# Weight-sum transfers of the seven-product groups, placed at written-out chunks of the load stream

## The chip, the cores and the metric

The kernel runs on one NeuronCore of a Trainium2 chip. The metric is the device time of one execution in microseconds (us). The engines that matter are TensorE (PE in the profile: matrix products and transposes), VectorE (DVE), ScalarE (ACT), GpSimd (POOL) and SyncE (SP). SP issues nearly all loads, POOL issues a few DMAs and computes the small powers of the norms. Each engine executes its own instructions in the order in which they were written, and waits for others by semaphores.

## The reference

Two decoder layers on 256 tokens of width 1024, all in float32. Layer 0 has a short gated convolution, attention over a memory of 256 rows, and a SwiGLU block; then one shared key and value projection. Layer 1 has block-sparse attention with these keys and values (with 256 tokens there is one block, so it is causal attention), memory attention, and SwiGLU.

```python
def mem_cross_attention(h, mem_n, w_q, w_kv, w_o):
    q = (h @ w_q).reshape(bsz, seq, MEM_HEADS, MEM_HEAD_DIM)
    k, v = jnp.split(mem_n @ w_kv, 2, axis=-1)
    ...
    return o @ w_o

def swiglu(h, w_gu, w_down):
    g, u = jnp.split(h @ w_gu, 2, axis=-1)
    return (jax.nn.silu(g) * u) @ w_down

def reference(...):
    for l in range(DEPTH):
        h = rms_norm(x, norm_mix[l])
        ...                      # short_conv_mixer or moba_attention, added to x
        x = x + mem_cross_attention(rms_norm(x, norm_mem[l]), rms_norm(mem, norm_memkv[l]), ...)
        x = x + swiglu(rms_norm(x, norm_ffn[l]), ffn_w_gu[l], ffn_w_down[l])
    return rms_norm(x, norm_final)
```

## The kernel before

**Products.** Every float32 product is made of three matmuls in a reduced format: each operand is split into a rounded part (hi) and the rest (lo), and lo x hi, hi x lo and hi x hi are added up in PSUM. Weights arrive as chunks of 128 x 1024 (512 KB). For each chunk SP loads raw_NAME, ACT casts it to hi_NAME, DVE subtracts to lo_NAME, and TensorE uses both. Names give the stage: memk, memv, mq and mo are the memory attention's key, value, query and output weights, k1, q1, v1 and o1 those of layer 1's attention, wr the row-wise pairs of the gate and up projection, wg, wu and wd its other pieces. There are five raw buffers (RAWS) and ten pairs of hi and lo (WBUFS), so the load of chunk n waits until lo of chunk n-5 is done.

**The load stream.** All chunks stand in one list, numbered from 0. Around the change: mo0 56 to 63, wr0 64 to 71, wg0 from 72; k1 136 to 143, q1 144 to 151, v1 152 to 159, memk1 160 to 167, o1 168 to 175, memv1 176 to 183, mq1 184 to 191, mo1 192 to 199, wr1 200 to 207, wg1 from 208. `Feed.load_to` issues the loads in this order, and just before chunk n it runs the functions that stand in `feed.hooks[n]`.

**What sets the order of the casts.** The kernel is written out by a planner, the class `Clock`. It holds one time for each engine and one for the DMA engines, and estimates when every tile is ready. `Feed.pump` is called between matmuls; it emits the hi cast of the next chunk on ACT (`split_high`) when the planner's time says that the raw chunk has landed and ACT is free, and then the lo subtraction on DVE (`split_low`). If `take` needs a chunk whose casts are not yet written, they are written there. So the planner's times decide nothing on the chip but the order of instructions on each engine.

**The sums.** Three of the eleven 256-wide pieces of the feed-forward layers (piece 8 of layer 0, pieces 4 and 8 of layer 1) are computed with seven products of quarter blocks in place of eight. For each, four sums of quarter blocks of the weight (T1 to T4, each in two parts i) are formed in DRAM by DMAs, in 16 steps: T1 <- B11, T3 <- B12 (plain copies), T1 += B12, T3 += B22 (accumulating DMAs), T2 <- T1 (copy), T2 += B22, T4 <- T2 (copy), T4 += B21. The plain copies are issued by SP (line 553), the accumulating ones by POOL (line 551). They are used much later, as chunks raw_wT. Each step also moves the planner's DMA time on, by 1460 ns for a copy and 3300 ns for an accumulate:

```python
            def run():
                clock.free["dma"] = max(clock.free["dma"], clock.now)
                if add:
                    nc.gpsimd.dma_start(dst, src, accum_op=OP.add, max_dma_last_dim=8192)
                else:
                    nc.sync.dma_start(dst, src)
                clock.note("dma", 3300 if add else 1460, [], [])
```

The steps are spread by `SUMS_AT` (loop at line 1041): the 16 of layer 0 evenly over chunks 44 to 104, the 32 of layer 1 evenly from chunk 128 on, the last ones drawn in to chunk 210.

Lines that the trace names: 242 is the helper that records every ACT, DVE and POOL operation, 464 the matmul, 468 the transpose, 481 the load of a chunk, 551 and 553 the accumulate and the copy of a sum, 1641 the load of the memory's transposed rows (mT, kept aside in DRAM, issued by POOL), 763 the first tile used to warm TensorE up.

Of the kernel before, what the change touches and what calls it, by code (L numbers as in the profile page):

```python
# [43 lines left out]
LATER = 2000  # L44
BANKWISE = 5
GROUPS = ((8,), (4, 8))
SUMS_AT = ((44, 104, 104), (128, 220, 210))


class Rows:  # L50
# [348 lines left out]
def yoco_kernel(  # L399
# [135 lines left out]
    def sum_steps(l, jp):  # L535
        for name in ("T1", "T2", "T3", "T4"):
            for i in range(2):
                weight_sums[l, jp, name, i] = aside.tile([P, 2, 2 * T], F32, name=f"{name}_{l}_{jp}_{i}")

        def step(name, source, i, add):  # L540
            dst = weight_sums[l, jp, name, i]
            if source[0] == "T":
                src = weight_sums[l, jp, source, i]
            else:
                n = quarters[l, jp, source, i]
                src = chunks[n * P:(n + 1) * P].rearrange("p (a n) -> p a n", a=2)
# [9 lines that stand above are left out]
            return run  # L556

        order = (("T1", "B11", False), ("T3", "B12", False), ("T1", "B12", True), ("T3", "B22", True),
                 ("T2", "T1", False), ("T2", "B22", True), ("T4", "T2", False), ("T4", "B21", True))
        return [step(name, source, i, add) for name, source, add in order for i in range(2)]  # L560

    plan, _, quarters, ffn_steps = weight_plan()
    feed = side.feed = Feed(clock, plan, load_chunk, split_high, split_low)
# [475 lines left out]
        feed.hooks[36 + k] = [put_aside(k)]  # L1039

    for l in range(2):
        steps = [step for jp in GROUPS[l] for step in sum_steps(l, jp)]
        first, end, last = SUMS_AT[l]
        for n, step in enumerate(steps):
            at = min(first + (end - first) * n // len(steps), last + n - len(steps))
            feed.hooks.setdefault(at, []).append(step)


    def short_conv(act, into):
# [711 lines left out]
```

## Time and profile before

| what | value |
|---|---|
| three runs | 783.0, 783.08, 783.8 us (median 783.08) |
| profiled execution | 783.51 us |
| its span, first to last instruction | 781.7 us |
| mean granted TensorE clock | 0.998 |
| DMA, mean over the span | 234 GB/s, 182.71 MB |
| accumulates of sums (POOL), each | 512 KB, 7.6 us from issue to landing, 24 of them |
| copies of sums (SP), each | 512 KB, 7.1 us (from the weights) and 5.4 us (T from T), 12 of each |

The page is read from the busy times down: which engine is nearly always busy, what it waited for, and then the stretches (windows of 10 us) in which the moved work lies. A row of the timeline gives start, duration, engine, line, operation, output and inputs, the count of instructions drawn together (the duration is then that of all), and in brackets the idle time before it with what ended it. Rows overlap slightly, since an instruction may start before the one ahead has written everything back.

### The profile page before, as it was taken

How to read it: one execution, taken by the hardware profiler on the slowest of the kernel's cores; microseconds unless marked ns; L12 is line 12 of the kernel's file. 1: busy time of each engine (PE TensorE's matmuls, PEld its weight loads, DVE VectorE, ACT ScalarE, POOL GpSimd, SP SyncE). 2: the span in 40 equal slices, each digit the busy share in tenths (PEclk: the TensorE clock that was granted, in tenths of full speed). 3: DMA queues.
4: the chain of work that ended last, by engine and by line, in shares of the span. 5: the costliest groups of instructions: out<-in, count | busy, mean ns of one | idle time of the engine just before them, and what ended most of it. 6: DMA issues, size and time to landing. Idle time of an engine off the chain costs nothing.

```text
span 781.7 us, 11230 instructions
## 1 busy us (share of the span) xinstructions
PE 773.4 (99%) x4147; PEld 665.0 (85%) x4147; DVE 573.6 (73%) x872; ACT 458.8 (59%) x728; POOL 36.8 (5%) x68
## 2 busy tenths in 40 slices
PE   9999999999999999999999999999999999999996
PEld 8988888898888888888888889888988888888885
DVE  6988888768786566687766566876867876966964
ACT  6875665665654555566564563655756556655741
POOL 1000011000100000000110010030000000000000
PEclk9999999999999999999999999999999999999999
DMA  9776888916676755699787556899674646946931
GB/s 345 277 275 214 275 287 230 372 67 212 193 245 232 226 174 205 207 366 330 217 306 243 188 161 218 294 266 310 208 224 151 241 158 226 321 164 211 345 111 54
DMA packets 48807, 182.71 MB, mean 234 GB/s; under 512 B 6256, under 2 KB 7280, under 8 KB 46576
## 3 DMA queue, kind: packets, MB, share of 16 engines
q1 hardware_dynamic: 45968, 166.79, 59.7%
q0 software_dynamic: 2208, 14.68, 9.2%
q8 instruction: 32, 0.52, 0.3%
q10 hardware_dynamic: 576, 0.52, 0.2%
q14 instruction: 23, 0.19, 0.1%
HBM read 178.82 MB, written 28.31 MB: 265 GB/s over the span
## 4 chain that ended last, share of the span: by engine, by line
PE 95%; DVE 1%; issue 0%; ACT 0%; POOLq 0%; DVEq 0%; ACTq 0%
PE gu L464 17%; PE ff L464 15%; PE seven L464 7%; PE q_acc L464 6%; PE cu L464 6%; PE rows L464 6%; PE acc_mo L464 6%; PE acc_memv L464 6%; PE acc_memk L464 4%; PE pb L464 3%; PE acc_v L464 3%; PE acc_q L464 3%; PE acc_o L464 3%; PE acc_cout L464 3%; PE acc_k L464 3%; PE po L464 2%
## 5 line engine op out<-in xcount | busy, mean ns | idle before, releaser
L464 PE MATMUL ff<-hi_wd,guT 128*128 128x512 f32 (+1 forms) x352 | 108.2, 388 | 0.0
L464 PEld LDWEIGHTS ff<-hi_wd,guT 128*128 128x128 f32 x352 | 65.8, 188 | 12.8
L464 PE MATMUL ff<-lo_wd,guT 128*128 128x512 f32 (+1 forms) x176 | 68.3, 388 | 0.0
L242 DVE TENSOR_TENSOR gu_sb<-gu_sb,gu 128x256 f32<-128x256 f32 x48 | 19.9, 421 | 58.7 <-ACT gu_sb L242 58.0
L242 DVE TENSOR_TENSOR lo_wd<-raw_wd,hi_wd 128x1024 fp32r<-128x1024 f32 x44 | 53.5, 1221 | 2.9 <-ACT hi_wd L242 2.7
L242 ACT COPY gu_sb<-gu 128x256 f32<-128x256 f32 x48 | 17.8, 372 | 61.4 <-PE gu L464 61.3
L242 ACT CAST hi_wd<-raw_wd 128x1024 fp32r<-128x1024 f32 x44 | 46.1, 1050 | 11.3 <-DMA raw_wd<-in_chunks_dram 9.4
L464 PE MATMUL gu<-ffn,hi_wg 128*128 128x512 f32 x192 | 48.0, 390 | 0.0
L464 PE MATMUL gu<-ffn,hi_wu 128*128 128x512 f32 x192 | 47.6, 390 | 0.0
L464 PE MATMUL acc_memk<-mT,hi_memk 128*128 128x256 f32 x256 | 44.3, 291 | 0.0
L242 ACT CAST hi_wu<-raw_wu 128x1024 fp32r<-128x1024 f32 x32 | 33.5, 1051 | 15.2 <-DMA raw_wu<-in_chunks_dram 10.9
L464 PEld LDWEIGHTS gu<-ffn,hi_wg 128*128 128x128 f32 x192 | 35.9, 188 | 7.3
L464 PEld LDWEIGHTS gu<-ffn,hi_wu 128*128 128x128 f32 x192 | 35.8, 188 | 7.3
L464 PE MATMUL rows<-hi_wr,ffn 128*128 128x512 f32 x128 | 40.7, 395 | 0.0
L464 PE MATMUL acc_mo<-hi_mo,oT_mem 128*128 128x512 f32 x128 | 40.6, 393 | 0.0
L464 PE MATMUL acc_memv<-hi_memv,mT 128*128 128x512 f32 x128 | 39.6, 390 | 0.0
L242 DVE TENSOR_TENSOR lo_wu<-raw_wu,hi_wu 128x1024 fp32r<-128x1024 f32 x32 | 38.9, 1221 | 0.6 <-ACT hi_wu L242 0.5
L464 PEld LDWEIGHTS acc_memk<-mT,hi_memk 128*128 128x128 f32 x256 | 38.8, 199 | 0.4 <-ACT hi_memk L242 0.3
L464 PEld LDWEIGHTS ff<-lo_wd,guT 128*128 128x128 f32 x176 | 33.2, 188 | 6.2
L242 POOL TENSOR_TENSOR rs<-ms,neg_half 128x1 f32<-128x1 f32 x14 | 13.5, 964 | 436.6 <-DVE ms L242 420.2
L464 PE MATMUL q_acc<-mem,hi_mq 128*128 128x512 f32 x128 | 32.4, 394 | 0.0
L242 DVE TENSOR_TENSOR lo_wg<-raw_wg,hi_wg 128x1024 fp32r<-128x1024 f32 x24 | 28.7, 1221 | 4.0 <-ACT hi_wg L242 3.9
(277 smaller groups left out, 1954.6 us busy)
## 6 DMA issues: line engine op xcount, KB each, us to landing
raw_wd<-in_chunks_dram SPq DMA_DIRECT2D x44, 512.0 KB, 4.9
raw_wu<-in_chunks_dram SPq DMA_DIRECT2D x32, 512.0 KB, 5.0
T<-in_chunks_dram POOLq DMA_DIRECT2D x24, 512.0 KB, 7.6
raw_wg<-in_chunks_dram SPq DMA_DIRECT2D x24, 512.0 KB, 5.0
raw_wT<-T SPq DMA_DIRECT2D x24, 512.0 KB, 4.7
raw_wB<-in_chunks_dram SPq DMA_DIRECT2D x18, 512.0 KB, 5.0
raw_memv<-in_chunks_dram SPq DMA_DIRECT2D x16, 512.0 KB, 4.7
raw_mq<-in_chunks_dram SPq DMA_DIRECT2D x16, 512.0 KB, 6.0
```

The lines of the kernel that those rows point to most:

```text
L242: return call(out, *args, **kw)
L464: nc.tensor.matmul(o, l, r, start=start, stop=stop)
```

## The change

`SUMS_AT` becomes a table of chunk numbers, one for each of the 16 steps of a group, and the loop reads it.

```diff
-SUMS_AT = ((44, 104, 104), (128, 220, 210))
+SUMS_AT = {
+    (0, 8): (65,) * 8 + (74, 77, 81, 85, 89, 92, 96, 100),
+    (1, 4): (128, 131, 134, 137, 140, 143, 146, 148) + (159,) * 4 + (166,) * 4,
+    (1, 8): (168,) * 8 + (201, 201, 202, 202, 206, 207, 208, 209),
+}
...
     for l in range(2):
-        steps = [step for jp in GROUPS[l] for step in sum_steps(l, jp)]
-        first, end, last = SUMS_AT[l]
-        for n, step in enumerate(steps):
-            at = min(first + (end - first) * n // len(steps), last + n - len(steps))
-            feed.hooks.setdefault(at, []).append(step)
+        for jp in GROUPS[l]:
+            for at, step in zip(SUMS_AT[l, jp], sum_steps(l, jp)):
+                feed.hooks.setdefault(at, []).append(step)
```

In layer 0 the first eight steps of piece 8 (four copies, four accumulates) now stand together before chunk 65. In layer 1 the second half of piece 4 stands before chunks 159 and 166, and the first eight steps of piece 8 before chunk 168. Lines shift by four in the changed kernel (242 becomes 246, 464 becomes 468, 481 becomes 485, 551 and 553 become 555 and 557).

On SP, around the first chunks of wr0, the order was this (the last two loads of mo0, then wr0; a number behind a name counts tiles):

```order
L481 DMA raw_mo0_6_1747<-in_chunks_dram 128x1024 [waits DMAHW1_49,DVE_49]
L481 DMA raw_mo0_7_1806<-in_chunks_dram 128x1024 [waits DMAHW2_49,DVE_49]
L481 DMA raw_wr0_0_0_1851<-in_chunks_dram 128x1024 [waits DMAHW3_49,DVE_49,Activation_49]
L481 DMA raw_wr0_0_1_2045<-in_chunks_dram 128x1024 [waits DMAHW5_49,DVE_49,Activation_49]
L481 DMA raw_wr0_0_2_2099<-in_chunks_dram 128x1024 [waits DMAHW6_49,DVE_49,Activation_49]
```

and is now this:

```order
L485 DMA raw_mo0_7_1800<-in_chunks_dram 128x1024 [waits DMAHW6_49,DVE_49]
L485 DMA raw_wr0_0_0_1845<-in_chunks_dram 128x1024 [waits DMAHW7_49,DVE_49,Activation_49]
L557 DMA T1_0_8_0_495<-in_chunks_dram 16x8192
L557 DMA T1_0_8_1_496<-in_chunks_dram 16x8192
L557 DMA T3_0_8_0_499<-in_chunks_dram 16x8192 [waits DMAHW0_49]
L557 DMA T3_0_8_1_500<-in_chunks_dram 16x8192 [waits DMAHW1_49]
L485 DMA raw_wr0_0_1_2047<-in_chunks_dram 128x1024 [waits DMAHW2_49,DVE_49,Activation_49]
L485 DMA raw_wr0_0_2_2100<-in_chunks_dram 128x1024 [waits DMAHW3_49,DVE_49,Activation_49]
```

The four copies, which stood between earlier loads, now stand behind the first load of wr0.

On DVE, at the end of layer 0's memory attention, where the residual rows (x_sb) are normed (ms, hn) for the feed-forward block, the order was this, from the third lo cast of wr0 on:

```order
L242 TENSOR_TENSOR lo_wr0_0_2_2187<-raw_wr0_0_2_2099,hi_wr0_0_2_2186 128x1024 [waits DMAHW3_49,Activation_49]
L242 TENSOR_TENSOR lo_wr0_0_3_2194<-raw_wr0_0_3_2112,hi_wr0_0_3_2193 128x1024 [waits DMAHW4_49,Activation_49]
L242 TENSOR_TENSOR oT_mem0_1_1706<-po_2200,oT_mem0_1_1706 128x2x256 [waits Activation_49]
L242 TENSOR_TENSOR lo_wr0_1_0_2226<-raw_wr0_1_0_2148,hi_wr0_1_0_2225 128x1024 [waits DMAHW5_49,Activation_49]
L242 TENSOR_TENSOR lo_wr0_1_1_2233<-raw_wr0_1_1_2176,hi_wr0_1_1_2232 128x1024 [waits DMAHW6_49,Activation_49]
L242 TENSOR_TENSOR x_sb_107<-x_sb_107,acc_mo0_0_0_2051 128x512 [waits PE_49]
L242 TENSOR_TENSOR x_sb_107<-x_sb_107,acc_mo0_0_1_2056 128x512 [waits PE_49]
L242 TENSOR_SCALAR msp_2274<-ss_2261 128x1 [waits Activation_49]
L242 TENSOR_SCALAR ms_2276<-ss_2261,msp_2274 128x1 [waits DVE_49,Activation_49]
L242 SCALAR_TENSOR_TENSOR hn_2287<-x_sb_107,rs_2273,g_ffn0_1708 128x512 [waits Pool_49]
```

and is now this, from the residual sum on:

```order
L246 TENSOR_TENSOR x_sb_107<-x_sb_107,acc_mo0_0_0_2053 128x512 [waits PE_49]
L246 TENSOR_TENSOR x_sb_107<-x_sb_107,acc_mo0_0_1_2058 128x512 [waits PE_49]
L246 TENSOR_SCALAR msp_2245<-ss_2230 128x1 [waits Activation_49]
L246 TENSOR_SCALAR ms_2247<-ss_2230,msp_2245 128x1 [waits DVE_49,Activation_49]
L246 TENSOR_TENSOR lo_wr0_0_1_2241<-raw_wr0_0_1_2047,hi_wr0_0_1_2240 128x1024 [waits DMAHW2_49,Activation_49]
L246 SCALAR_TENSOR_TENSOR hn_2261<-x_sb_107,rs_2244,g_ffn0_1703 128x512 [waits DMAHW0_49,Pool_49]
L246 SCALAR_TENSOR_TENSOR hn_2263<-x_sb_107,rs_2244,g_ffn0_1703 128x512
L246 TENSOR_TENSOR x_sb_107<-x_sb_107,acc_mo0_1_0_2160 128x512 [waits PE_49]
L246 TENSOR_TENSOR ffn0_0_2222<-pt_h_2275,ffn0_0_2222 128x4x128 [waits Activation_49]
L246 TENSOR_TENSOR x_sb_107<-x_sb_107,acc_mo0_1_1_2170 128x512 [waits PE_49]
L246 TENSOR_TENSOR ffn0_1_2223<-pt_h_2281,ffn0_1_2223 128x4x128 [waits Activation_49]
L246 TENSOR_TENSOR lo_wr0_0_2_2258<-raw_wr0_0_2_2100,hi_wr0_0_2_2257 128x1024 [waits DMAHW3_49]
```

lo_wr0_0_2 to lo_wr0_1_1 stood ahead of the residual sum, and lo_wr0_0_1 ahead of those; now lo_wr0_0_1 stands between ms and hn, and lo_wr0_0_2 behind both ffn casts.

On ACT, where layer 1's attention ends (pT1, oT_moba) and the keys of its memory attention (k_sb, memk1_u) are cast, the order was this:

```order
L242 COPY pT1_4878<-pt1_4873 128x512 [waits PE_49,Activation_49]
L242 CAST oT_moba_1_4430<-po1_4891 128x2x128 [waits PE_49]
L242 CAST hi_o1_0_4918<-raw_o1_0_4847 128x1024 [waits DMAHW5_49]
L242 CAST hi_o1_1_4938<-raw_o1_1_4883 128x1024 [waits DMAHW6_49]
L242 CAST hi_o1_2_4963<-raw_o1_2_4900 128x1024 [waits DMAHW7_49]
L242 CAST memk1_u0_5006<-k_sb_5008 128x2x256 [waits DVE_49]
L242 CAST hi_o1_3_5028<-raw_o1_3_4914 128x1024 [waits DMAHW0_49]
L242 CAST memk1_u0_5006<-k_sb_5023 128x2x256 [waits DVE_49]
L242 CAST hi_o1_4_5053<-raw_o1_4_4928 128x1024 [waits DMAHW1_49]
L242 CAST hi_o1_5_5064<-raw_o1_5_4946 128x1024 [waits DMAHW2_49,PE_49]
```

and is now this:

```order
L246 COPY pT1_4887<-pt1_4882 128x512 [waits PE_49,Activation_49]
L246 CAST oT_moba_1_4426<-po1_4900 128x2x128 [waits PE_49]
L246 CAST memk1_u0_4995<-k_sb_4997 128x2x256 [waits DVE_49]
L246 CAST memk1_u0_4995<-k_sb_5012 128x2x256 [waits DVE_49]
L246 CAST hi_o1_0_5042<-raw_o1_0_4850 128x1024 [waits DMAHW1_49]
L246 CAST hi_o1_1_5053<-raw_o1_1_4892 128x1024 [waits DMAHW2_49]
L246 CAST memk1_u1_5027<-k_sb_5049 128x2x256 [waits DVE_49]
L246 CAST memk1_u1_5027<-k_sb_5051 128x2x256 [waits DVE_49]
L246 CAST hi_o1_2_5070<-raw_o1_2_4909 128x1024 [waits DMAHW3_49]
L246 CAST hi_o1_3_5077<-raw_o1_3_4922 128x1024 [waits DMAHW4_49]
```

hi_o1_0 to hi_o1_2 stood ahead of the first memk1_u cast; now hi_o1_0 and hi_o1_1 stand behind two of them, and hi_o1_2 behind four.

On DVE, at the same place, the order was this:

```order
L242 SCALAR_TENSOR_TENSOR lo_memk1_7_4796<-raw_memk1_7_4672,g_cols_106,hi_memk1_7_4795 128x1024 [waits DMAHW4_49]
L242 TENSOR_TENSOR lo_o1_0_4919<-raw_o1_0_4847,hi_o1_0_4918 128x1024 [waits DMAHW5_49,Activation_49]
L242 TENSOR_TENSOR lo_o1_1_4939<-raw_o1_1_4883,hi_o1_1_4938 128x1024 [waits DMAHW6_49,Activation_49]
L242 TENSOR_TENSOR lo_o1_2_4964<-raw_o1_2_4900,hi_o1_2_4963 128x1024 [waits DMAHW7_49,Activation_49]
L242 TENSOR_TENSOR k_sb_5008<-acc_memk1_0_4725,m_rsb_105 128x512 [waits PE_49]
L242 TENSOR_TENSOR k_sb_5023<-acc_memk1_1_4726,m_rsb_105 128x512 [waits PE_49]
L242 TENSOR_TENSOR memk1_u0_5006<-k_sb_5008,memk1_u0_5006 128x2x256 [waits Activation_49]
L242 TENSOR_TENSOR lo_o1_3_5029<-raw_o1_3_4914,hi_o1_3_5028 128x1024 [waits DMAHW0_49,Activation_49]
L242 TENSOR_TENSOR memk1_u0_5006<-k_sb_5023,memk1_u0_5006 128x2x256 [waits Activation_49]
L242 TENSOR_TENSOR lo_o1_4_5054<-raw_o1_4_4928,hi_o1_4_5053 128x1024 [waits DMAHW1_49,Activation_49]
L242 TENSOR_TENSOR k_sb_5078<-acc_memk1_2_4727,m_rsb_105 128x512 [waits PE_49]
```

and is now this:

```order
L246 SCALAR_TENSOR_TENSOR lo_memk1_7_4873<-raw_memk1_7_4668,g_cols_106,hi_memk1_7_4872 128x1024 [waits DMAHW4_49]
L246 TENSOR_TENSOR k_sb_4997<-acc_memk1_0_4721,m_rsb_105 128x512 [waits PE_49]
L246 TENSOR_TENSOR k_sb_5012<-acc_memk1_1_4722,m_rsb_105 128x512 [waits PE_49]
L246 TENSOR_TENSOR memk1_u0_4995<-k_sb_4997,memk1_u0_4995 128x2x256 [waits Activation_49]
L246 TENSOR_TENSOR memk1_u0_4995<-k_sb_5012,memk1_u0_4995 128x2x256 [waits Activation_49]
L246 TENSOR_TENSOR lo_o1_0_5043<-raw_o1_0_4850,hi_o1_0_5042 128x1024 [waits DMAHW1_49,Activation_49]
L246 TENSOR_TENSOR k_sb_5049<-acc_memk1_2_4723,m_rsb_105 128x512 [waits PE_49]
L246 TENSOR_TENSOR k_sb_5051<-acc_memk1_3_4724,m_rsb_105 128x512 [waits PE_49]
L246 TENSOR_TENSOR lo_o1_1_5054<-raw_o1_1_4892,hi_o1_1_5053 128x1024 [waits DMAHW2_49,Activation_49]
L246 TENSOR_TENSOR memk1_u1_5027<-k_sb_5049,memk1_u1_5027 128x2x256 [waits Activation_49]
L246 TENSOR_TENSOR memk1_u1_5027<-k_sb_5051,memk1_u1_5027 128x2x256 [waits Activation_49]
L246 TENSOR_TENSOR lo_o1_2_5071<-raw_o1_2_4909,hi_o1_2_5070 128x1024 [waits DMAHW3_49,Activation_49]
```

lo_o1_0 to lo_o1_2 stood ahead of the first k_sb; now lo_o1_0 stands behind two k_sb and two memk1_u0, lo_o1_1 behind two more k_sb, and lo_o1_2 behind two memk1_u1. TensorE's order from the last matmuls of acc_memk1 to the first of acc_o1 is the same in both.

## The prediction

> **What bounds the kernel now.** I read the page's busy times first, then what TensorE waited for, then windows, and only then the rows around the moved work.
>
> ```profile
> span 781.7 us, 11230 instructions
> PE 773.4 (99%) x4147; PEld 665.0 (85%) x4147; DVE 573.6 (73%) x872; ACT 458.8 (59%) x728; POOL 36.8 (5%) x68
> ...
> PE 95%; DVE 1%; issue 0%; ACT 0%; POOLq 0%; DVEq 0%; ACTq 0%
> ```
>
> TensorE is busy for 773.4 of 781.7 us and 95% of the chain that ended last is TensorE's. The list of everything that it waits for has two lines, both from the start of the program (the second falls between 20 and 30 us):
>
> ```profile
> PE warm L464 <- DVE blank L763: 1.5, 1, 1.5
> PE acc_memk L464 <- DVE lo_memk L242: 0.4, 1, 0.4
> ```
>
> So no weight transfer ends a TensorE wait anywhere. The windows (columns: window, then length, then the busy time of PE, PEld, DVE, ACT, POOL, then granted clock, DMA share, GB/s) say the same of the stretches that the change touches:
>
> ```profile
> 160.00:170.00 10.00, 10.00 (x72) 9.28 (x71) 6.13 (x15) 6.99 (x16) 0.00 (x0) 1.00 0.01 2
> 200.00:210.00 10.00, 10.00 (x49) 8.09 (x48) 8.08 (x12) 7.24 (x12) 2.22 (x2) 1.00 0.44 95
> 380.00:390.00 10.00, 9.93 (x48) 7.93 (x47) 8.44 (x13) 7.61 (x11) 2.48 (x4) 1.00 0.86 210
> 390.00:400.00 10.00, 9.92 (x49) 7.92 (x48) 4.62 (x12) 4.10 (x5) 1.61 (x2) 1.00 0.78 317
> 460.00:470.00 10.00, 10.00 (x76) 9.41 (x74) 5.15 (x15) 6.43 (x15) 0.00 (x0) 1.00 0.46 120
> 490.00:500.00 10.00, 10.00 (x50) 8.46 (x49) 9.55 (x11) 6.81 (x8) 0.00 (x0) 1.00 0.77 251
> ```
>
> Two things follow. Idle TensorE time that could be won is 0.4 us at the start plus 0.07 and 0.08 us in the two windows from 380 to 400, some 0.6 us in all, 0.07%. And every microsecond by which a weight comes late in one of these full windows is paid in full, since nothing later has slack to take it back. The moved transfers themselves go where the DMA engines are nearly idle (share 0.01 and 0.46), so they are not what will cost. What will is the order of the casts.
>
> **The change, part by part.** Nothing is added or removed: each engine executes the same instructions. Each of the 48 steps keeps its queue (copies on SP, accumulates on POOL). But a step also advances the planner's DMA clock, by 1.46 us a copy and 3.3 us an accumulate. Eight steps before one chunk advance it by 4 x 1.46 + 4 x 3.3 = 19 us, so the planner believes that the next chunk lands 19 us later, and writes that chunk's two casts (hi on ACT, lo on DVE) further down its engines' orders. The engines execute in that order, although the raw chunk is there early. The two places where it matters are those of eight steps: chunk 65 and chunk 168.
>
> Place one, chunk 65 (wr0_0_1, the first projection of the row pairs). Before, four lo_wr casts stood ahead of the norm; now lo_wr0_0_1 stands between ms and hn, and the casts behind it are late as well.
>
> ```profile
> 196.12 1.03 ACT L242 CAST hi_wr<-raw_wr 128x1024 fp32r<-128x1024 f32 x1
> 199.17 0.59 ACT L242 CAST ffn<-pt_h 128x512 fp32r<-128x512 f32 x1 [2.02 <-PE pt_h L468]
> ...
> 197.14 1.41 DVE L242 SCALAR_TENSOR_TENSOR hn<-x_sb,rs,g_ffn 128x512 f32<-128x512 f32 x2 [0.68 <-POOL rs L242]
> 199.79 0.69 DVE L242 TENSOR_TENSOR ffn<-pt_h,ffn 128x512 fp32r<-128x512 f32 x1 [0.64 <-ACT ffn L242]
> 202.67 1.22 DVE L242 TENSOR_TENSOR lo_wr<-raw_wr,hi_wr 128x1024 fp32r<-128x1024 f32 x1
> ...
> 200.80 0.39 PE L464 MATMUL rows<-lo_wr,ffn 128*128 128x512 f32 x1
> 201.03 0.62 PE L464 MATMUL rows<-hi_wr,ffn 128*128 128x512 f32 x2
> ```
>
> Step by step: hi_wr0_0_1 takes the slot of the hi_wr at 196.12, ready 197.15. lo_wr0_0_1 (1.22) fills 197.2 to 198.4, and hn, which could start at 197.14, starts at 198.35: 1.2 us late. TensorE's transposes of hn were planned four matmuls later (4 x 0.23 us), so they wait for nothing, but the ffn cast moves from 199.17 to about 200.1 and its DVE half from 199.79 to 200.70, ending at 201.39. TensorE wants that half at 201.03: **0.4 us** of waiting. The second token half repeats it: its rs (1.45 us on POOL) starts after two more late lo_wr casts on DVE, hn comes at 205.55 against 204.33, and lo_wr0_1_0 behind it ends at 208.2. In TensorE's shifted time it wants the transposes at 206.2 (ready 206.3) and lo_wr0_1_0 some 0.35 us before it is there. That is 0.1 + 0.35, together **0.9 us** for the place. The loads behind (the five raw buffers come free with the lo casts, so raw_wr0_1_3 issues at about 204) land 3 us or more before their use. Bounds: the first wait alone, less half of it, 0.2; all three with one more cast's quarter, 1.6.
>
> Place two, chunk 168 (o1_0, the output projection of layer 1's attention). Before, three lo_o casts were done at 484; now lo_o1_0 stands behind two k_sb and two memk_u instructions that wait for matmuls.
>
> ```profile
> 480.52 3.49 DVE L242 TENSOR_TENSOR lo_o<-raw_o,hi_o 128x1024 fp32r<-128x1024 f32 x3
> ...
> 488.30 0.69 DVE L242 TENSOR_TENSOR k_sb<-acc_memk,m_rsb 128x512 f32<-128x512 f32 x1 [0.75 <-PE acc_memk L464]
> 488.90 0.68 DVE L242 TENSOR_TENSOR memk_u<-k_sb,memk_u 128x512 fp32r<-128x512 f32 x1
> 489.50 1.22 DVE L242 TENSOR_TENSOR lo_o<-raw_o,hi_o 128x1024 fp32r<-128x1024 f32 x1
> ...
> 477.66 2.13 ACT L242 CAST hi_o<-raw_o 128x1024 fp32r<-128x1024 f32 x2
> 489.06 0.62 ACT L242 CAST memk_u<-k_sb 128x512 fp32r<-128x512 f32 x1
> 489.58 1.99 ACT L242 CAST hi_o<-raw_o 128x1024 fp32r<-128x1024 f32 x2
> ...
> 490.98 0.40 PE L464 MATMUL acc_o<-lo_o,oT_moba 128*128 128x512 f32 x1
> 491.21 0.62 PE L464 MATMUL acc_o<-hi_o,oT_moba 128*128 128x512 f32 x2
> ...
> 492.36 0.39 PE L464 MATMUL acc_o<-lo_o,oT_moba 128*128 128x512 f32 x1
> ```
>
> The second k_sb cannot start before 488.30, because it waits for TensorE. Then the memk_u cast runs on ACT to 489.68, hi_o1_0 goes into the slot at 489.58 and ends at 490.62, and lo_o1_0 fills 490.65 to 491.87. TensorE wants it at 490.98, so it starts at 491.93: **0.95 us**. One chunk feeds TensorE for 492.36 - 490.98 = 1.38 us, so it wants lo_o1_1 at 493.30; DVE first does the next two k_sb (0.6 us apart, to 493.0) and lo_o1_1 to 494.2: **0.95 us**. It wants lo_o1_2 at 495.6; DVE has two memk_u (to 495.4) and lo_o1_2 to 496.55: **0.95 us**. From lo_o1_3 on casts follow each other at 1.14 us against TensorE's 1.38, and catch up; o1_7, whose raw buffer comes free only with lo_o1_2, may cost another 0.1. Sum **2.9 us**. Bounds: two waits, 1.9; the three with a loaded landing of o1_6 and o1_7 (half a us each), 3.9.
>
> What I cost at nothing. At chunks 128 to 159 the casts of v1_7 and the memk1 chunks move behind some softmax steps; by the same walk these are done 0.3 us or more before use, bounds 0 and 0.5. In the mo1 and wr1 stage some transposes stand one to four matmuls elsewhere, and from wr1_1_0 on the orders agree again, bounds -0.2 and 0.4. POOL: mT1_1 now stands behind the two T4 accumulates, and rs for o1 behind four T1 and T3 accumulates.
>
> ```profile
> 453.70 0.55 POOL L1641 DMA_DIRECT2D mT<-mem_aside  x1 [43.02 <-ACT hi_memk L242]
> ...
> 510.30 1.47 POOL L242 TENSOR_TENSOR rs<-ms,neg_half 128x1 f32<-128x1 f32 x1 [54.30 <-DVE ms L242]
> ...
> T<-in_chunks_dram POOLq DMA_DIRECT2D x24, 512.0 KB, 7.6
> ...
> T<-T SPq DMA_DIRECT2D x12, 512.0 KB, 5.4
> ```
>
> The T4 copies issue with the memk1_6 load (about 455), land 5.4 us later, and mT1_1 follows two accumulate issues, near 463; TensorE reaches mT1's second half near 479. The four accumulates are done 30 us before the rs at 510. If that cover were gone, mT1_1 late by one more accumulate landing (7.6) would still be in time. SP waits for copies in no place that I find. Gains: no more than the 0.6 us above, and none of it beside a moved step, so 0.
>
> The sum goes against the profiled execution's own time, 783.51 us (span 781.7 and 1.8 around it), which lies 0.4 above the median of the three runs, 783.08: 0.9 + 2.9 = 3.8, so 787.3 in a profile and **786.9** as a median.
>
> On transfers, the Trainium skill, "DMA: Bandwidth & Descriptors", section "Issuing engines are not separate DMA queues", says that DMAs of SP, ACT and POOL run on the same 16 engines and interleave. By that rule what is bunched at chunk 168 would lengthen the raw_o loads beside it; a sum that took raw_o two landings late would still be 3.8, because raw_o1_0 lands by 479 before and is now not cast until 489.58. The rows at 160 to 170 and at 460 to 470 show why it is left out.
>
> **Rivals.**
> (a) The o1 waits do not come, and the time does not change. Place: ACT's hi_o1_0. It decides whether k_sb1, at 488.30 before, comes 0.95 us or more earlier relative to the first acc_o. If it did, the two later waits would go as well (DVE would have its k_sb and memk_u behind it), and 0.9 of place one would remain at most: 783.08 + 0.9 = 784.0, inside 0.2%. Against it: TensorE's order from the last acc_memk to the first acc_o is unchanged, and the 0.75 us before k_sb are a wait on exactly that. For it: my walk takes every instruction in its old duration. 10%.
> (b) Follow-on costs: the DVE and ACT orders stay late beyond the places that I walked (raw buffers free late, so loads late, so casts late), worth another one to three waits of 0.95, 788 to 790. For it: DVE is busy 9.55 of 10 us from 490 to 500. Against: from lo_o1_3 on it gains 0.24 us a chunk. 12%.
> (c) The clock drops under the repeated waits. The start of the trace shows what that costs:
>
> ```profile
> 4.23 3.44 PE L464 MATMUL acc_memk<-mT,hi_memk 128*128 128x256 f32 x16
> ...
> 483.77 0.40 PE L464 MATMUL acc_memk<-mT,hi_memk 128*128 128x256 f32 x2
> 484.01 0.28 PE L464 MATMUL acc_memk<-mT,lo_memk 128*128 128x256 f32 x1
> 484.13 0.40 PE L464 MATMUL acc_memk<-mT,hi_memk 128*128 128x256 f32 x2
> ```
>
> Sixteen matmuls took 3.44 us there, where three take 484.13 - 483.77 = 0.36 us later, so 1.92 for sixteen: 1.5 us more for one such stretch, 788.4. Against it: the end of the program, where
>
> ```profile
> 776.00:778.00 2.00, 0.00 (x0) 0.00 (x0) 1.53 (x7) 0.51 (x1) 0.60 (x1) 1.00 0.00 0
> ```
>
> two whole us without a matmul still had clock 1.00. The Trainium skill, "TensorE: Matmul & The Clock Gate", section "A second HAM failure mode: psum-queue depth-cycling", tells of a kernel whose small idle gaps between groups were frequent enough to make the clock go back and forth; that would be this case, and no wait of this trace is like it. 4%.
> (d) Faster: some transfer that I do not see on the path is relieved. The 0.6 us above bound it, under 0.2%. 1%.
>
> **How the numbers follow.** Forecast with its own bounds, 0.2 to 1.6 and 1.9 to 3.9, less 0.2 and more 0.9 for the small parts: 783.08 + 1.9 to 783.08 + 6.4 at the extremes, and the ends of all would not meet; 785.2 to 788.4 holds most of its 73%. To reach 8 in 10 the range takes in half of (b) and (c) and a little of (a): 784.8 to 789.4. A measurement of this kernel tells about 0.2%, 1.6 us, from no change. Slower by more: 73 + 12 + 4 = 89%; I give 0.86, since some of the forecast's low end lies at 1.9. Same 0.12, faster 0.02.
>
> **What would show it.** TensorE's waits would name DVE lo_o three times with about 0.9 us each, and DVE ffn and lo_wr with 0.3 to 0.5; hi_o1_0 on ACT would start at about 489.6 plus place one's loss; the windows near 201 to 210 would show PE 9.1 and those near 491 to 498 together 2.9 us short; all other windows full, with transfers in 160 to 175 and 455 to 475. Wrong would be: full windows at both places (the casts were early after all), a wait on mT or rs (POOL's order), or a granted clock under 1.00 after 491.

## The result, and the profile after

Five runs of the changed kernel gave 788.18 to 789.9 us, median 789.34, beside 783.08 for the kernel before (782.98 to 783.88 in the same session). The ratio of the means is 1.0073, 95% interval 1.0059 to 1.0088: slower by 6.3 us between the medians and 5.7 us between the means, where 3.8 were forecast. The profiled execution took 788.53 us.

The page of the changed kernel, with the chain that ended last:

```profile
span 786.7 us, 11217 instructions
PE 774.7 (98%) x4147; PEld 664.0 (84%) x4147; DVE 573.2 (73%) x872; ACT 457.7 (58%) x728; POOL 36.8 (5%) x68
...
PE 90%; DMA 3%; DVE 2%; ACT 1%; issue 1%; POOL 0%; POOLq 0%; DVEq 0%; ACTq 0%; SPq 0%
```

TensorE's work is as it was (774.7 us against 773.4), and the span is 5.0 us longer. The list of what TensorE waited for has new lines:

```profile
PE acc_o L468 <- DVE lo_o L246: 2.2, 3, 0.9
PE warm L468 <- DVE blank L767: 1.5, 1, 1.5
PE gu L468 <- DVE gu_sb L246: 0.8, 1, 0.8
PE pt_g L472 <- DVE gg L246: 0.5, 1, 0.5
PE acc_memk L468 <- DVE lo_memk L246: 0.4, 2, 0.2
PE rows L468 <- DVE ffn L246: 0.2, 1, 0.2
PE rows L468 <- DVE lo_wr L246: 0.2, 1, 0.2
```

lo_o, ffn and lo_wr were forecast; gu for gu_sb and pt_g for gg were not. In the windows (PE busy is the first number after the window's length), four stretches behind the start lost time. The first and the last were full before (10.00 each in the prediction's rows); so were the other two, which these rows show, first of before and then, behind the dots, of the changed kernel:

```profile
220.00:230.00 10.00, 10.00 (x54) 8.51 (x53) 8.36 (x12) 5.39 (x8) 0.00 (x0) 1.00 0.86 288
260.00:270.00 10.00, 10.00 (x54) 8.62 (x53) 5.75 (x8) 2.83 (x6) 0.00 (x0) 1.00 0.81 294
...
200.00:210.00 10.00, 9.52 (x45) 7.17 (x44) 9.16 (x13) 8.92 (x14) 1.45 (x1) 1.00 0.51 163
220.00:230.00 10.00, 9.49 (x46) 7.71 (x45) 5.66 (x9) 4.35 (x7) 0.54 (x1) 1.00 1.00 329
260.00:270.00 10.00, 9.21 (x48) 7.63 (x47) 5.75 (x8) 4.36 (x7) 0.00 (x0) 1.00 0.91 311
490.00:500.00 10.00, 7.84 (x46) 6.24 (x45) 9.20 (x12) 7.95 (x11) 0.00 (x0) 1.00 0.36 109
```

A wait in the list, and a gap in a window, is shorter than what it costs: in a full stretch of before a matmul of 0.39 us starts at 200.80 and the next one already at 201.03, so the recorded end lies 0.16 us behind the start of the next. So I also took the start of the n-th matmul in both traces and subtracted. This table is worked out from the traces; a column gives by how many us each kernel is behind the profiled execution of before when that one stands at the time in the first column (runs differ by up to 0.4 from the start on, so the steps between rows are what counts):

```
time in before   changed  told only  moved only  168 only  65 only  T2,T4 away  told of 159  half told
195                -0.4      -0.0        0.4        0.2      -0.2       0.0          0.6        -0.2
224                 0.6       1.1        0.4        0.2       1.0       1.1          0.6         0.9
240                 1.4       2.0        0.4        0.2       1.9       1.1          0.6         1.7
275                 2.6       3.3        0.4        0.2       1.9       1.1          0.6         3.1
420                 2.1       2.9        0.6        0.2       1.8       1.2          0.9         2.8
488                 2.2       2.9        2.9        0.2       1.9       1.2          1.0         2.8
497                 5.1       5.9        3.0        3.1       1.9       4.2          1.0         2.8
770                 5.0      10.8        3.3        3.1       1.9       4.2          1.0         3.3
```

The changed kernel's column is the loss by place: 1.0 at the row pairs (195 to 224), 0.8 at 230, 1.1 at 268, 0.4 regained between 380 and 400 (where before has its own two small gaps), 3.0 at o1. The other columns are the experiments.

At the row pairs, TensorE and DVE of the changed kernel:

```profile
201.04 0.73 PE L468 MATMUL rows<-hi_wr,ffn 128*128 128x512 f32 x2 [0.23 <-DVE ffn L246]
207.87 0.50 PE L468 MATMUL rows<-lo_wr,ffn 128*128 128x512 f32 x1 [0.17 <-DVE lo_wr L246]
...
196.66 1.23 DVE L246 TENSOR_TENSOR lo_wr<-raw_wr,hi_wr 128x1024 fp32r<-128x1024 f32 x1 [0.73 <-ACT hi_wr L246]
197.81 1.41 DVE L246 SCALAR_TENSOR_TENSOR hn<-x_sb,rs,g_ffn 128x512 f32<-128x512 f32 x2
200.29 0.69 DVE L246 TENSOR_TENSOR ffn<-pt_h,ffn 128x512 fp32r<-128x512 f32 x1 [0.48 <-ACT ffn L246]
```

lo_wr0_0_1 lies between ms and hn, and the ffn half that it delays ends at 200.98, just ahead of the matmul at 201.04. The pair of matmuls behind this wait takes 0.73 us, where the same pair took 0.62 in before, so a wait also costs 0.11 us behind it. At o1, DVE, then ACT, then TensorE:

```profile
490.46 0.69 DVE L246 TENSOR_TENSOR k_sb<-acc_memk,m_rsb 128x512 f32<-128x512 f32 x1 [0.75 <-PE acc_memk L468]
492.79 1.22 DVE L246 TENSOR_TENSOR lo_o<-raw_o,hi_o 128x1024 fp32r<-128x1024 f32 x1 [0.26 <-ACT hi_o L246]
...
491.71 1.99 ACT L246 CAST hi_o<-raw_o 128x1024 fp32r<-128x1024 f32 x2
...
494.16 0.47 PE L468 MATMUL acc_o<-lo_o,oT_moba 128*128 128x512 f32 x1 [0.86 <-DVE lo_o L246]
496.40 0.50 PE L468 MATMUL acc_o<-lo_o,oT_moba 128*128 128x512 f32 x1 [0.61 <-DVE lo_o L246]
498.74 0.50 PE L468 MATMUL acc_o<-lo_o,oT_moba 128*128 128x512 f32 x1 [0.68 <-DVE lo_o L246]
```

hi_o1_0 starts at 491.71, the forecast 489.58 and the 2.1 us that the kernel was behind by then; lo_o1_0 follows it, and each of three chunks starts late.

The two places that no step of the prediction has are in layer 0's feed-forward block. ACT, DVE, TensorE and POOL of the changed kernel there (the rows of POOL are accumulates of T2 and T4):

```profile
228.06 1.05 ACT L246 CAST hi_wg<-raw_wg 128x1024 fp32r<-128x1024 f32 x1 [1.43 <-DMA raw_wg<-in_chunks_dram]
229.01 0.37 ACT L246 ACTIVATE sg<-rows 128x256 f32<-128x256 f32 x1
...
229.42 0.42 DVE L246 TENSOR_TENSOR gg<-rows,sg 128x256 f32<-128x256 f32 x1 [0.93 <-ACT sg L246]
...
229.90 0.44 PE L472 MATMUL pt_g<-ident,gg 128*128 128x128 f32 x2 [0.51 <-DVE gg L246]
...
266.71 1.05 ACT L246 CAST hi_wu<-raw_wu 128x1024 fp32r<-128x1024 f32 x1 [3.96 <-DMA raw_wu<-in_chunks_dram]
267.66 0.64 ACT L246 COPY gu_sb<-gu 128x256 f32<-128x256 f32 x2
...
268.54 2.14 PE L468 MATMUL gu<-ffn,hi_wg 128*128 128x512 f32 x8 [0.79 <-DVE gu_sb L246]
...
214.11 0.82 POOL L555 DMA_DIRECT2D T<-in_chunks_dram  x1 [8.88 <-DMA T<-T]
219.76 0.78 POOL L555 DMA_DIRECT2D T<-in_chunks_dram  x1 [4.83 <-DMA T<-T]
...
258.08 0.79 POOL L555 DMA_DIRECT2D T<-in_chunks_dram  x1 [4.25 <-DMA T<-T]
```

ACT executes in the written order: the cast that waits for its raw chunk holds what stands behind it, sg for gg in the one case (sg starts at 229.01, when the cast of 228.06 is done), the copy that empties gu's bank in the other (267.66, behind the cast of 266.71). In the kernel before, the same cast of wu waited less:

```profile
262.71 1.05 ACT L242 CAST hi_wu<-raw_wu 128x1024 fp32r<-128x1024 f32 x1 [2.29 <-DMA raw_wu<-in_chunks_dram]
...
254.70 0.79 POOL L551 DMA_DIRECT2D T<-in_chunks_dram  x1 [4.92 <-DMA T<-T]
```

Its load was issued 3.5 us behind the last accumulate (254.70, issued at 258.19), in the changed kernel 1.5 us behind it (258.08, at 259.62), and was there for its cast 7.1 us after its issue instead of 4.5. The wg chunk cast at 228.06 was issued at 218.03, 10.0 us earlier, between the accumulates of 214.11 and 219.76. These two stand at the same chunks as before, but were issued at 204.25 and 215.20 there: the load stream came late, and took them along. So three theories were left to tell apart: that the late casts alone cost, that the bunched transfers cost by themselves, and that some waits need both.

### The profile page after: what moved, and what is told of

Same layout as the page of the kernel before. It is cut to its first block, busy times and chain, and to the rows that moved or that the text cites. A ratio compares the mean times of both kernels' runs of the same rounds, so it can differ in the third digit from the quotient of the medians.

```text
span 786.7 us, 11217 instructions
## 1 busy us (share of the span) xinstructions
PE 774.7 (98%) x4147; PEld 664.0 (84%) x4147; DVE 573.2 (73%) x872; ACT 457.7 (58%) x728; POOL 36.8 (5%) x68
## 4 chain that ended last, share of the span: by engine, by line
PE 90%; DMA 3%; DVE 2%; ACT 1%; issue 1%; POOL 0%; POOLq 0%; DVEq 0%; ACTq 0%; SPq 0%
PE gu L468 16%; PE ff L468 14%; PE seven L468 7%; PE q_acc L468 6%; PE cu L468 6%; PE acc_memv L468 6%; PE acc_mo L468 6%; PE acc_memk L468 3%; PE pb L468 3%; PE acc_v L468 3%; PE rows L468 3%; PE acc_q L468 3%; PE acc_k L468 3%; PE acc_cout L468 3%; PE acc_o L468 2%; PE po L468 2%
## 5 line engine op out<-in xcount | busy, mean ns | idle before, releaser
L555 POOL DMA_DIRECT2D T<-in_chunks_dram x24 | 19.2, 812 | 308.6 <-DMA T<-T 163.7
```

## The experiments

The planner's part and the transfers can be separated: a step has a function that issues the DMA and one that tells the planner, and each is hung at a chunk of its own.

```diff
-            def run():
-                clock.free["dma"] = max(clock.free["dma"], clock.now)
+            def run():
                 if add: ...
+            def tell():
+                clock.free["dma"] = max(clock.free["dma"], clock.now)
                 clock.note("dma", 3300 if add else 1460, [], [])
-            return run
+            return run, tell
...
+            for at, told, (run, tell) in zip(SUMS_AT[l, jp], TOLD_AT[l, jp], sum_steps(l, jp)):
+                feed.hooks.setdefault(at, []).append(run)
+                feed.hooks.setdefault(told, []).append(tell)
```

In the traces, "moved only" has before's order of instructions on ACT, DVE and TensorE row for row, and "told only" and "T2 and T4 away" have the changed kernel's. The ratios (of means) below are against runs of before on the same chip (median 783.76 for the first four kernels, 783.61 for the last four).

**Told only**: `SUMS_AT` of before, `TOLD_AT` of the change.

> The transfers stand at the chunks of before; only the planner is told of them at the chunks of the change. ACT, DVE and TensorE then have, row for row, the order of the changed kernel. Theory (the late casts cost, not the transfers): the waits of the changed kernel appear without its transfers: three waits of TensorE for lo_o of 0.9 us each, the waits for ffn and lo_wr of about 0.9 together, and some of what the changed kernel lost between 220 and 270 us: 787 to 789. Rival (the bunched transfers cost, by contention or by blocked queues): no wait for lo_o, 783 within 0.8.

Measured: 793.97 us median, ratio 1.0133 (1.0117 to 1.0148), 10.2 us slower, and so beyond what either theory gave. TensorE's waits:

```profile
PE acc_o L473 <- DVE lo_o L251: 3.4, 4, 1.2
...
PE gu L473 <- DVE gu_sb L251: 1.0, 1, 1.0
PE pt_h L477 <- DVE x_sb L251: 0.9, 1, 0.9
PE pt_g L477 <- DVE gg L251: 0.6, 1, 0.6
```

All waits of the changed kernel are there without its moved transfers (the T2 and T4 accumulates of layer 0 stand at the same chunks in both). There is a fourth wait for lo_o besides, and more behind it: of its 10.8 us in the table 5 come after 497. The four plain copies of the third group (T1 and T3) are issued between the loads of o1 and memv1 there (SP at 495 to 511), where the raw buffers now come free late, and the late loads land later still: ACT waits for raw_o1_7 until 6.0 us after its issue, where 3.3 were enough in the changed kernel. So the late order costs, and having moved the transfers out of that stretch saves a part of it, since the changed kernel has the same order and loses nothing after 497. Only the first 2.6 of the 5 us (497 to 505) were followed to these copies.

**Moved only**: `SUMS_AT` of the change, `TOLD_AT` of before.

> The transfers stand at the chunks of the change, and the planner is told of them at the chunks of before, so ACT, DVE and TensorE have the order of before. Theory (late casts): 783.1 within 0.8, no TensorE wait for lo_o, lo_wr or ffn. Rival (bunched transfers): 786 to 789. A gain of over 1 us would say that the new places are better by themselves and only the planner's reaction costs; at most 0.6 us of idle TensorE time is there to be won.

Measured: 786.78 us, ratio 1.004 (1.0027 to 1.0053), 3.0 us slower. None of the three waits by late casts came, as the first theory has it, but its time was missed, and the rival's was met: there is one large new wait, pt_r for r, 2.3 us in the table (the other steps, near 399 and 749, are 0.2 and 0.3). ACT there, POOL and TensorE, and in the last line the same cast of raw_v1_7 in before:

```profile
433.94 1.15 ACT L251 ACTIVATE hi_v<-raw_v,g_cols 128x1024 fp32r<-128x1024 f32 x1 [2.74 <-DMA raw_v<-in_chunks_dram]
434.99 0.67 ACT L251 ACTIVATE r<-acc_q,rs 128x512 f32<-128x512 f32 x1
...
422.60 0.82 POOL L559 DMA_DIRECT2D T<-in_chunks_dram  x1 [31.01 <-DMA T<-T]
423.67 0.78 POOL L559 DMA_DIRECT2D T<-in_chunks_dram  x1 [0.26 <-PE pt_r L477]
...
436.73 0.63 PE L477 MATMUL pt_r<-ident,r 128*128 128x128 f32 x4 [2.15 <-DVE r L251]
...
430.60 1.16 ACT L242 ACTIVATE hi_v<-raw_v,g_cols 128x1024 fp32r<-128x1024 f32 x1
```

The two T2 accumulates of chunk 159 are issued at 422.60 and 423.67, raw_v1_7 at 425.50, and its cast starts at 433.94, 8.4 us later; in before it was issued at 424.92 and cast at 430.60, without a wait, so it had landed within 5.7 us. r stands behind the cast, and TensorE waits for r. In the changed kernel the planner had been told, hi_v1_7 stands behind r, and this wait is not there. So the bunched transfers do delay a load, and telling the planner of them is what hides it at this place.

**168 only**: the third group as in the change, the other two as in before, for transfers and planner alike.

> Only the places of the second group of layer 1 (168 and 201 to 209) are those of the change, the other two groups stand as before. Theory: the three waits for lo_o, 2.9 us, and nothing before 480 us: 786.0 (785.3 to 786.7). If the losses of the two places are not independent (the early one moving the later one), the sum would be off by more than 0.7.

Measured: 786.45 us, ratio 1.0034 (1.0022 to 1.0047), 2.7 us. Its waits for lo_o are 2.2 us in three, as in the changed kernel, and the table has one step, 3.0 us between 488 and 497. The o1 term stands by itself.

**T2 and T4 away**: the changed kernel, told as the changed kernel, with `(65,) * 8 + (66, 67, 68, 69, 98, 100, 102, 104)` for the transfers of layer 0's group.

> The changed kernel, with the order of ACT, DVE and TensorE unchanged, but the eight later transfers of layer 0's group (T2, T4) taken out of the stretch from 205 to 265 us: T2 to chunks 66 to 69, T4 to 98 to 104. Theory one for the two waits that the forecast did not have (pt_g for gg at 230 us, gu for gu_sb at 268 us): a weight load that is late anyway meets an accumulating transfer; then both waits go, 1.3 to 1.9 us less than the changed kernel, 787.5. Theory two: the loads are late because their raw buffers come free late, and transfers have no part; then both waits stay and the time is that of the changed kernel, 789.3.

Measured: 787.64 us (787.31 to 787.73), ratio 1.0049 (1.0036 to 1.0062), 1.7 us under the changed kernel's 789.34 and outside its runs (2.4 if each is taken against before in its own session, 6.3 and 3.9). Of the waits these are left, and the two for gu_sb and gg went:

```profile
PE acc_o L473 <- DVE lo_o L251: 2.2, 3, 0.9
...
PE rows L473 <- DVE ffn L251: 0.2, 1, 0.2
...
PE rows L473 <- DVE lo_wr L251: 0.2, 1, 0.2
```

Theory one holds: in the order of before the same transfers cost nothing at 230 and 268 (moved only), and with the late order nothing either when they are elsewhere. It takes both. The loads show it too: the wu chunk was there 3.2 us after its issue (259.32 to 262.51) instead of 7.1, the wg chunk within 6.5 (218.27 to 224.74) instead of 10.0. What is left is 3.9 us against before, the two places that the forecast had.

**Told of 159 only**: all transfers as in the change; `TOLD_AT` as in the change for layer 1's first group, as in before for the others.

> All transfers at the places of the change; the planner is told of layer 1's first group (128 to 166) where it stands, of the other two groups at the places of before. Theory (telling helps where a transfer really delays the next chunk, which is the case at 159, and harms where the chunk is there long before, which is the case at 65 and 168): hi_v1_7 stands behind the first r cast again, the wait of 2.2 us that the moved transfers alone caused at 435 us goes, the lo_o and lo_wr waits do not come: 783.6 (783.0 to 784.6), as before. Rival (the moved transfers cost in other places as well): 785 or more.

Measured: 784.25 us (782.79 to 784.52), ratio 1.0003 (0.9994 to 1.0012). No difference from before is shown: the wait at 435 is gone, as are those for lo_o and lo_wr. One thing was not as written: in the profiled execution TensorE lost 0.8 us near 182, where ACT's hi_wr0_0_1 waited for its chunk:

```profile
179.73 1.05 ACT L251 CAST hi_wr<-raw_wr 128x1024 fp32r<-128x1024 f32 x1 [2.16 <-DMA raw_wr<-in_chunks_dram]
```

It was issued at 173.30, 6.4 us earlier; in before the chunk was there within 4.2. So at 65, too, the bunched transfers delay the next chunk, but to about 180, not to the 195.6 at which the changed kernel casts it. Another 0.6 us was lost near 374, where ff waited for guT, and half of it came back by 400; its cause is open.

**Told of 159, T2 and T4 away**: the transfers of "T2 and T4 away", the planner told as in "told of 159 only".

> As the one told of 159 only, and the T2 and T4 transfers of layer 0's group taken out of the stretch from 205 to 265 us (chunks 66 to 69 and 98 to 104). Theory: at most 0.6 us can be won over before, since TensorE waits for nothing else there: 783.4 (782.6 to 784.2). If the transfers between 205 and 265 cost before something that no wait shows, it would be under 782.5.

Measured: 784.96 us (783.68 to 788.49), ratio 1.0017 (1.0006 to 1.0027): a little over the expected range, and nothing won. Its profiled execution lost 1.0 us between 150 and 190, where T2's accumulates now are. What made its slowest run 788.49 is open.

**65 only**: layer 0's group as in the change, the others as in before.

> Only layer 0's group stands as in the change. Theory: the waits for ffn and lo_wr near 201 to 208 us (0.95 together), and those near 230 and 268 us that need both late loads and the T2 and T4 transfers (0 to 1.9, differing from run to run): 784.7 to 786.6; nothing after 480 us. Rival (the two late waits belong to something else): 784.7 flat.

Measured: 785.43 us, ratio 1.0024 (1.0014 to 1.0034), 1.8 us. The table has 1.1 for the row pairs and 1.0 at 230, and the wait at 268 did not come in this execution, though it came in two others with the same order and transfers there. Here the wu load was issued 0.9 us behind the last accumulate (259.25, at 260.11) and was there 5.8 us later; in the two others it was issued 1.5 and 1.4 us behind it and took 7.1 and 7.4. So being nearer to the accumulate is not by itself worse; what decides the length of the load was not tried by itself.

**Half told**: the changed kernel, with half of 3300 and 1460 ns for layer 1's second group.

```diff
-                clock.note("dma", 3300 if add else 1460, [], [])
+                clock.note("dma", (3300 if add else 1460) * (0.5 if (l, jp) == (1, 8) else 1), [], [])
```

> The changed kernel; the planner is told of half the duration of each step of layer 1's second group. DVE's lo_o1_0 then stands behind one k_sb instead of two and two memk_u. By the same hand schedule lo_o1_0 is ready at 488.8 against 490.98, lo_o1_1 at 490.7 against 492.36, lo_o1_2 at 492.5 against 493.7: no wait for lo_o at all, 2.9 us less than the changed kernel (786.4; the late part before it is the changed kernel's). Rival (the o1 waits come from the raw loads beside the bunched transfers): they stay.

Measured: 786.82 us, ratio 1.0042 (1.0029 to 1.0055), 2.5 us under the changed kernel's median. There is no wait for lo_o; 0.5 us came in its place between 497 and 505. ACT, DVE and TensorE:

```profile
484.88 1.05 ACT L251 CAST hi_o<-raw_o 128x1024 fp32r<-128x1024 f32 x1 [4.30 <-DMA raw_o<-in_chunks_dram]
...
490.29 1.22 DVE L251 TENSOR_TENSOR lo_o<-raw_o,hi_o 128x1024 fp32r<-128x1024 f32 x1
...
493.80 0.40 PE L473 MATMUL acc_o<-lo_o,oT_moba 128*128 128x512 f32 x1
```

lo_o1_0 is done at 491.5, 2.3 us before its use, with the same eight transfers ahead of the same loads. So the o1 waits come from the order that the planner's number sets. The transfers do delay the load: raw_o1_0 was issued at 476.25 and ACT waited for it until 484.88, 8.6 us, where before it was there within 4.2 (473.45 to 477.66). That is at least 4.4 us, where the planner of the change books 19 and the one of this run 9.5; and the chunk is still cast 5.4 us before DVE takes it up.

## Why the prediction was right, and where it was short

**The bound.** Right: what came late was paid nearly in full. Of 5.9 us lost behind 195 in the profiled execution 0.4 came back between 380 and 400 (the spans differ by 5.0, since the changed kernel was 0.4 ahead at 195). There the windows of before had shown idle time of 0.07 and 0.08 us, so these, too, stood for more than they list. The median, 789.34, fell in the range by 0.06 us, and two of the five runs lie above its end, 789.4. It lies outside the band that the forecast's own mechanism was given, 785.2 to 788.4, and in that of rival (b), follow-on costs, 788 to 790. That the range held is owed to the share of (b) that was taken into it, and in part to luck.

**Place two.** Right in place, order and size: 2.85 us for three waits were forecast, 1.02, 0.86 and 0.98 were measured (the starts of acc_o, 494.16, 496.40 and 498.74 against 490.98, 492.36 and 493.72, less the 2.16 that the kernel was behind before). The 0.1 for o1_7 did not come. "168 only" shows it alone, "half told" takes it away.

**Place one.** Right in place and near in size: 0.9 was forecast, 1.0 measured. The first wait moved the matmul at 201.03 by the 0.4 that was forecast, and 0.1 went behind it. The second half's transposes cost nothing net, where 0.1 was forecast; lo_wr0_1_0 cost 0.5 with what went behind it, where 0.35 was.

**The step that failed** is the one sentence on the loads: that those behind place one land 3 us or more before their use. It was worked out as far as wr0_1_3 and held there. The loads after it, wg0, wu0 and wd0, also wait for raw buffers that come free late, and meet the T2 and T4 accumulates of the same group, which I had left out because their chunks are the same as before. Their times are not: T2's moved from 204 and 215 to 214 and 220, among the late loads. That cost 0.8 and 1.1 us in the profiled execution and 1.7 us between medians (T2 and T4 away). Rival (b) had this kind of loss, late buffers and so late loads and casts, at 12%, but argued it for o1 alone, behind which it did not come.

**"The moved transfers are not what will cost"** was true of the changed kernel only because the planner was told of them. At 159 they delay raw_v1_7 by enough to cost 2.3 us (moved only), and at 65 and 168 they delay the next chunk as well, which has time to spare there. I had read DMA shares at 160 to 170 and 460 to 470, but not around the load that follows the accumulates.

**POOL and SP.** Right: no wait for mT or rs. **Rival (c)**: the granted clock was 0.998 in both, and 1.00 in the window from 490 to 500, so no drop. **Rivals (a)** and **(d)**: the waits came, and no gain did. The profile's 5.0 us and the medians' 6.3 are not the same number; three of the five runs lie at 789.3 to 789.9 and two at 788.2 to 788.5, and the waits at 230 and 268, which came and went between kernels, could make such a difference. That was not shown for single runs. The signs forecast for the windows came smaller than written, 9.52 for 9.1 and 2.2 us short for 2.9, since a gap in a window lists less than the wait costs.

## What to carry to other kernels

When a kernel's order is set by a planner's clock, a change of where something is booked is first a change of order: compare the orders on each engine and walk the engines at each place where a cast has moved, and then follow the buffers and loads behind it until they are back on time, with all the other transfers of that stretch. Separate what is issued from what the planner is told, since the parts do not add up to the whole: here order alone cost 10.2 us, transfers alone 3.0, both together 6.3. A booking that is too long can cost as much as one that is missing: at chunk 168, 19 us were booked for a delay of at least 4.4, and that cost 3.0 us, where half the booking cost 0.5; at chunk 159 the missing booking cost 2.3.

## What the hardware showed

In these traces a load of 512 KB that was issued 1.4 to 3.1 us behind the last of one to four accumulating transfers of 512 KB was there 7.1 to 8.6 us after its issue (wu, raw_v1_7, raw_o1_0). The same loads took 3.2 to 4.5 us, or at most 4.2 and 5.7, where the accumulates were further off or absent. One load, issued 0.9 us behind an accumulate, took 5.8 (65 only). That a moved order with the old transfers would cost 10.2 us, four more than with the new ones, I had not expected.
